# Merging the 32x32 blocks of four heads' triangular inverses at once

## The chip, the cores and the metric

The kernel runs on one core of one Trainium2 chip. The metric is device time in microseconds of one execution, the median of three runs: 887.85 us for the kernel before (886.28 to 888.44).

## The reference

One layer of a bidirectional encoder block, 512 tokens wide 1024, float32. An input projection gives pooling channels, q, k, v, gates and decays; branch A pools, branch B runs a chunked gated delta rule forward and backward for 8 heads of width 128; both are gated, summed, projected and added to x, and a channel mixer (up-projection, convolution, SiLU gate, down-projection) follows. What matters here is the triangular solve of the delta rule:

```python
L = jnp.where(strict, jnp.einsum('bhnid,bhnjd->bhnij', kb, k) * decay, 0.0)
eye = jnp.eye(CHUNK, dtype=L.dtype)
rhs = jnp.concatenate([kb * jnp.exp(G)[..., None], vb], axis=-1)
sol = lax.linalg.triangular_solve(L + eye, rhs, left_side=True, lower=True,
                                  unit_diagonal=True)
```

For each head, direction and chunk a unit triangular matrix is inverted and applied.

## The kernel before

**Chunks and heads.** The kernel uses chunks of 128 tokens (`NT` = 4 of them) instead of 64. The heads form two groups of `HG` = 4. For a group, one tile `nm` of shape (128, 4 heads, 2 directions, 4 chunks, 128) holds the triangular matrices; the solve multiplies by their inverses from there.

**The inverse in three levels.** `mats_unit` (L828) builds the matrices and writes their 32x32 diagonal blocks to DRAM; `inv_unit` (L864) inverts all of a group's blocks at once; `spread_unit` (L925) loads the inverted blocks back, into `nm` and, transposed, into a second tile `ext`. Then `merge_unit` (L949) merges 32x32 blocks to 64x64 (level 1) and 64x64 to 128x128 (level 2). An off-diagonal block of the inverse is a product of three blocks, so each level has two rounds of small float32 matmuls with a copy between:

- `m1` (PE, L960) writes bank `l1a`; `x1` (ACT, L964) copies it to SBUF.
- `m2` (PE, L971) writes bank `l1b`, copied back into `nm` by `k2a` (ACT, L982 and L983) and `k2b` (DVE, L987 and L988).
- `m2t` (PE, L978) makes the transposed product in bank `l1t`; `k2t` (ACT L992, DVE L994) puts it into `ext`.
- `m3` (PE, L1010 and L1011) writes `l2a`; `x2_` (ACT, L1015) copies it.
- `m4` (PE, L1021 and L1022) writes `l2b`; `k4` (ACT L1026, DVE L1028) copies it into `nm`.

The unit is called once for each head. Its small matmuls use 32x32 or 64x64 corners of the PE array, so those of different corners run side by side.

**What follows.** `delta_unit` (L1086) runs the recurrence for two heads at a time: `solve` (L1137) is its first PE step and needs both heads' finished `nm`; its scalings (L1141) write buffers of the ring `x4`, three of which the unit takes at its start. `fin_unit` finishes a head.

**Order.** The program is written as tasks with an engine, a cost, the names they read and write, and a key. `Planner.run` (L88) plays the tasks in time with these costs and gives the order of instructions. On each engine the ready task with the lowest key goes first. Dependences across engines add 0.5 us ahead of PE and 0.2 elsewhere. Large projections (three 128x512 matmuls for a step, L371 to L373, `mm3`) have late keys, so they fill PE wherever the chain of the delta rule (`CHAIN` keys) has nothing ready. Costs of ACT and DVE copies come from `ca` and `cd` (L188, L192). Each engine then runs its list in order and waits on semaphores. SP starts most transfers, ACT those of `ext`.

**Buffers.** `RINGS` (L243) gives the buffers of each kind: `ds` are 3 PSUM banks of 512 columns for the small steps, `x4` 3 SBUF tiles of 1024 columns (the blocks of `inv_unit`, the states of `delta_unit`), `x1` and `x2` one each for the copies in a merge. Rings in the strict list are taken in the order of declaration.

Of the kernel before, what the change touches and what calls it, by code (L numbers as in the profile page):

```python
# [209 lines left out]
def hybrid_block(  # L210
# [23 lines left out]
    pe, act, dve, pool, sp = nc.tensor, nc.scalar, nc.vector, nc.gpsimd, nc.sync  # L234
# [345 lines left out]
    def w_cols(c0, n=P):  # L580
        return w_in[0][:, c0 : c0 + n]
# [185 lines left out]
    nms, exts, vs = [None] * H, [None] * H, [None] * H  # L767
    nmg, extg = [None] * 2, [None] * 2
# [56 lines left out]
    def nmn(h):  # L825
        return [f"nm:{h // HG}#h{h}{d}" for d in range(2)]
# [119 lines left out]
            L(128, lambda b_=b_: load(b_, False), r=[f"uscr{g}", f"bscr{g}", f"nm:{g}"], w=[f"nml{g}#{b_}"], key=c, land=4.0, issue=1.1)  # L946


    def merge_unit(h):  # L949
        g, c = h // HG, CHAIN + 1000 * (h // HG) + 600 + 10 * h  # L950
        b = {}
        q = [slice(i * B32, (i + 1) * B32) for i in range(4)]
        lo_, hi_ = slice(0, 64), slice(64, 128)
        def m1():
            b["p1"] = bank("ds", f"l1a_{h}")[:, 0 : NT * B32].rearrange("p (t c) -> p t c", c=B32)
            nm, ext = nms[h], exts[h]
            a, z = slice(0, 32), slice(32, 64)
            for t in range(NT):
                for o, i, d, e in ((1, 0, 0, a), (3, 2, 0, a), (0, 1, 1, z), (2, 3, 1, z)):
                    pe.matmul(b["p1"][q[o], t, :], nm[q[i], d, t, q[o]], ext[q[i], d, t, e], start=True, stop=True)  # L960

        def x1():
            b["x1"] = ring("dp", "x1", (P, NT, B32), F32, f"x1_{h}")
            act.copy(b["x1"], b["p1"])  # L964

        def m2():
            p = b["p2"] = bank("ds", f"l1b_{h}")[:, 0 : NT * B32].rearrange("p (t c) -> p t c", c=B32)
            nm, x1_ = nms[h], b["x1"]
            for t in range(NT):
                for o, i, d in ((0, 1, 0), (2, 3, 0), (1, 0, 1), (3, 2, 1)):  # L970
                    pe.matmul(p[q[o], t, :], x1_[q[i], t, :], nm[q[i], d, t, q[i]], start=True, stop=True)  # L971

        def m2t():
            p = b["p2t"] = bank("ds", f"l1t_{h}")[:, 0 : NT * B32].rearrange("p (t c) -> p t c", c=B32)
            nm, x1_ = nms[h], b["x1"]
            for t in range(NT):
                for o, d in ((1, 0), (2, 1)):
                    pe.matmul(p[q[o], t, :], nm[q[o], d, t, q[o]], x1_[q[o], t, :], start=True, stop=True)  # L978

        def k2a():  # L980
            nm, p = nms[h], b["p2"]
            act.copy(nm[q[0], 0, :, q[1]], p[q[0]])  # L982
            act.copy(nm[q[2], 0, :, q[3]], p[q[2]])  # L983

        def k2b():
            nm, p = nms[h], b["p2"]
            dve.tensor_copy(nm[q[1], 1, :, q[0]], p[q[1]])  # L987
            dve.tensor_copy(nm[q[3], 1, :, q[2]], p[q[3]])  # L988

        def k2t(d):  # L990
            if d == 0:
                act.copy(exts[h][q[1], 0, :, 0:32], b["p2t"][q[1]])  # L992
            else:
                dve.tensor_copy(exts[h][q[2], 1, :, 32:64], b["p2t"][q[2]])  # L994

        nm_n, ext_n = nmn(h), [f"ext:{g}#{h}0", f"ext:{g}#{h}1"]
        M(0.75, m1, r=[*nm_n, *ext_n, f"exl{g}", f"nml{g}"], w=[f"ds:l1a{h}", f"x1:{h}"], key=c)
        A(ca(128), x1, r=[f"ds:l1a{h}"], w=[f"x1:{h}"], key=c)
        M(0.6, m2, r=[*nm_n, f"x1:{h}"], w=[f"ds:l1b{h}"], key=c)
        M(0.45, m2t, r=[*nm_n, f"x1:{h}"], w=[f"ds:l1t{h}"], key=c)  # L1000
        A(2 * ca(128), k2a, r=[f"ds:l1b{h}"], w=[nm_n[0]], key=c)
        V(2 * cd(128), k2b, r=[f"ds:l1b{h}"], w=[nm_n[1]], key=c)
        A(ca(128), lambda: k2t(0), r=[f"ds:l1t{h}"], w=[ext_n[0]], key=c)
        V(cd(128), lambda: k2t(1), r=[f"ds:l1t{h}"], w=[ext_n[1]], key=c)

        def m3():
            pv = b["p3"] = bank("ds", f"l2a_{h}")[:, 0:256].rearrange("p (t c) -> p t c", c=64)
            nm, ext = nms[h], exts[h]
            for t in range(NT):
                pe.matmul(pv[hi_, t, :], nm[lo_, 0, t, hi_], ext[lo_, 0, t, :], start=True, stop=True)  # L1010
                pe.matmul(pv[lo_, t, :], nm[hi_, 1, t, lo_], ext[hi_, 1, t, :], start=True, stop=True)  # L1011

        def x2_():
            b["x2"] = ring("dp", "x2", (P, NT, 64), F32, f"xl2_{h}")
            act.copy(b["x2"], b["p3"])  # L1015

        def m4():
            pv = b["p4"] = bank("ds", f"l2b_{h}")[:, 0:256].rearrange("p (t c) -> p t c", c=64)
            nm = nms[h]
            for t in range(NT):  # L1020
                pe.matmul(pv[lo_, t, :], b["x2"][hi_, t, :], nm[hi_, 0, t, hi_], start=True, stop=True)  # L1021
                pe.matmul(pv[hi_, t, :], b["x2"][lo_, t, :], nm[lo_, 1, t, lo_], start=True, stop=True)  # L1022

        def k4(d):
            if d == 0:
                act.copy(nms[h][lo_, 0, :, hi_], b["p4"][lo_])  # L1026
            else:
                dve.tensor_copy(nms[h][hi_, 1, :, lo_], b["p4"][hi_])  # L1028

        M(0.7, m3, r=[*nm_n, *ext_n], w=[f"ds:l2a{h}", f"x2:{h}"], key=c)  # L1030
        A(ca(256), x2_, r=[f"ds:l2a{h}"], w=[f"x2:{h}"], key=c)
        M(0.7, m4, r=[*nm_n, f"x2:{h}"], w=[f"ds:l2b{h}"], key=c)
        A(ca(256), lambda: k4(0), r=[f"ds:l2b{h}"], w=[nm_n[0]], key=c)
        V(cd(256), lambda: k4(1), r=[f"ds:l2b{h}"], w=[nm_n[1]], key=c)
# [388 lines left out]
    gbox, gpp, _ = job(w_cols(C_GATE, 32), KD, hx, hr, "gate", halves=True, pair=True)  # L1423
# [48 lines left out]
    x2 = [None] * NT  # L1472
# [214 lines left out]
    for c in range(NF):  # L1687
        b = {}
# [19 lines left out]
        else:  # L1708
            i = c - HK
# [255 lines left out]
```

## Time and profile before

| what | value |
|---|---|
| median of three runs | 887.85 us (886.28, 887.85, 888.44) |
| span of the profiled execution | 887.7 us (no other time of it is listed) |
| PE busy | 876.2 us, 99%, 5179 matmuls |
| DVE, ACT, POOL busy | 548.2, 462.1, 499.7 us |
| merges of group 0, first to last matmul and a little after | 163.7 to 188.1 us |
| merges of group 1 | 345.6 to 368.1 us |
| bytes read and written in HBM | 114.08 and 25.20 MB |

The profile is of one execution. Busy time counts instructions in flight; PE records matmuls, PEld weight loads, which overlap them. Matmuls are pipelined, so a large one shows 0.39 us while the next starts 0.23 us after it: durations on PE are read from start to start. A row of the timeline has start, duration, engine, line, operation, output and inputs, tile of the array, shape and count; brackets give the idle time before it and what ended that.

### The profile page before, as it was taken

What the parts mean: (1) busy time and instruction counts of PE and PEld (TensorE: products, weight loads), DVE (VectorE), ACT (ScalarE), POOL (GpSimd) and SP (SyncE); (2) the same over time, 40 slices, a digit from 0 to 9 for tenths busy, and PEclk for the clock granted to TensorE, in tenths of its full rate; (3) what the DMA queues carried; (4) which work ended last, traced back from release to release, by engine and by line L of the source; (5) the groups of instructions that cost most, each with busy time, mean ns of one, the idle gap of its engine ahead of it and who ended that gap; (6) DMA issues with size and microseconds to landing.
All of it is one profiled execution on the core that took longest, in us unless ns stands there. A gap on an engine that the chain in (4) does not pass through costs nothing. (4 is left out here: it accounts for less than half of the span.)

```text
span 887.7 us, 14092 instructions
## 1 busy us (share of the span) xinstructions
PE 876.2 (99%) x5179; PEld 737.7 (83%) x5179; DVE 548.2 (62%) x981; ACT 462.1 (52%) x791; POOL 499.7 (56%) x446
## 2 busy tenths in 40 slices
PE   8999999999999999999999999999999999999997
PEld 7988888788988887889878888888888888888886
DVE  5756687157777795555534244666655454569996
ACT  5688644435877444334854333444443333465664
POOL 3445555214556554243667905777788764567763
PEclk9999999999999999999999999999999999999999
DMA  7365545813344559112898606566766653366554
GB/s 207 87 204 141 131 120 163 148 25 112 91 134 117 143 148 150 43 49 81 254 291 265 191 21 210 194 215 218 241 214 202 236 168 100 115 194 197 167 172 159
DMA packets 176265, 140.20 MB, mean 158 GB/s; under 512 B 32110, under 2 KB 143547, under 8 KB 176196
## 3 DMA queue, kind: packets, MB, share of 16 engines
q1 hardware_dynamic: 167298, 137.20, 51.3%
q10 hardware_dynamic: 8898, 2.10, 1.6%
q8 instruction: 41, 0.67, 0.3%
q14 instruction: 28, 0.23, 0.1%
HBM read 114.08 MB, written 25.20 MB: 157 GB/s over the span
## 5 line engine op out<-in xcount | busy, mean ns | idle before, releaser
L396 POOL TENSOR_TENSOR wl_up<-wr_up,wh_up 128x512 fp32r<-128x512 f32 x88 | 115.0, 1328 | 49.3 <-ACT wh_up L392 49.2
L372 PE MATMUL ps_up<-h_lo,wh_up 128*128 128x512 f32 (+1 forms) x368 | 139.9, 380 | 0.3 <-DVE h_lo L541 0.3
L371 PE MATMUL ps_up<-h_hi,wh_up 128*128 128x512 f32 (+1 forms) x368 | 139.9, 380 | 0.0
L373 PE MATMUL ps_up<-h_hi,wl_up 128*128 128x512 f32 (+1 forms) x368 | 139.7, 380 | 0.0
L1678 DVE SCALAR_TENSOR_TENSOR c<-ps_up,fw,c 128x511 f32<-128x511 f32 x88 | 66.0, 750 | 100.0 <-ACT c L1672 94.1
L1663 POOL TENSOR_TENSOR tp<-tp 128x512 f32<-128x512 f32 x44 | 59.9, 1361 | 42.6 <-DMA tp<-in_ffn_down_dram 37.0
L1867 POOL TENSOR_TENSOR w_dn<-wr_dn,w_dn 128x512 fp32r<-128x512 f32 x44 | 66.1, 1515 | 28.5 <-ACT w_dn L1864 27.1
L372 PEld LDWEIGHTS ps_up<-h_lo,wh_up 128*128 128x128 f32 x368 | 69.2, 188 | 13.8 <-DVE h_lo L541 0.5
L373 PEld LDWEIGHTS ps_up<-h_hi,wl_up 128*128 128x128 f32 x368 | 69.2, 188 | 13.2
L371 PEld LDWEIGHTS ps_up<-h_hi,wh_up 128*128 128x128 f32 x368 | 69.2, 188 | 13.0
L392 ACT CAST wh_up<-wr_up 128x1024 fp32r<-128x1024 f32 x44 | 46.2, 1050 | 61.4 <-issue 29.3
L1864 ACT CAST w_dn<-wr_dn 128x512 fp32r<-128x512 f32 x69 | 42.4, 621 | 29.6 <-PE dn L373 21.1
L372 PE MATMUL dn<-w_dn,as 128*128 128x512 f32 x141 | 54.2, 385 | 0.0
L371 PE MATMUL dn<-w_dn,as 128*128 128x512 f32 x141 | 54.2, 384 | 0.0
L373 PE MATMUL dn<-w_dn,as 128*128 128x512 f32 x141 | 54.2, 384 | 0.0
L1632 DVE TENSOR_TENSOR as<-a,as 128x512 fp32r<-128x512 f32 (+1 forms) x41 | 41.8, 1044 | 0.1
L1628 ACT CAST as<-a 128x512 fp32r<-128x512 f32 (+1 forms) x41 | 21.5, 535 | 33.5 <-DVE a L1699 29.8
L396 POOL TENSOR_TENSOR wl_gp<-wr_gp,wh_gp 128x512 fp32r<-128x512 f32 x16 | 21.2, 1348 | 25.6 <-ACT wh_gp L392 25.6
L1672 ACT ACTIVATE c<-ps_up,fw 128x512 f32<-128x512 f32 x44 | 33.9, 770 | 0.0
L1701 ACT ACTIVATE c<-c 128x512 f32<-128x512 f32 x22 | 13.9, 633 | 35.0 <-DVE c L1678 35.0
L396 POOL TENSOR_TENSOR wl_do<-wr_do,wh_do 128x512 fp32r<-128x512 f32 x16 | 25.7, 1627 | 11.1 <-ACT wh_do L392 10.8
L396 POOL TENSOR_TENSOR wl_v<-wr_v,wh_v 128x512 fp32r<-128x512 f32 x16 | 20.5, 1304 | 19.8 <-ACT wh_v L392 19.8
(362 smaller groups left out, 2440.7 us busy)
## 6 DMA issues: line engine op xcount, KB each, us to landing
wr_up<-in_ffn_up_dram SPq DMA_DIRECT2D x44, 512.0 KB, 4.0
tp<-in_ffn_down_dram SPq DMA_DIRECT2D x22, 512.0 KB, 5.4
t_scr<-tp SPq DMA_DIRECT2D x44, 256.0 KB, 2.9
wr_dn<-t_scr SPq DMA_DIRECT2D x20, 512.0 KB, 3.9
wr_dn<-in_ffn_down_dram SPq DMA_DIRECT2D x15, 512.0 KB, 3.6
x<-in_x_dram SPq DMA_DIRECT2D x8, 512.0 KB, 5.4
wr_k<-in_w_in_dram SPq DMA_DIRECT2D x8, 512.0 KB, 6.5
wr_z<-in_w_in_dram SPq DMA_DIRECT2D x8, 512.0 KB, 3.9
```

Of the source, the lines that this page charges most:

```text
L371: pe.matmul(ps, ahi, bhi, start=first, stop=False)
L372: pe.matmul(ps, ahi, blo, start=False, stop=False)
L373: pe.matmul(ps, alo, bhi, start=False, stop=last)
L392: act.copy(b["hi"], b["raw"])
L396: pool.tensor_tensor(out=b["lo"][:, sl], in0=b["raw"][:, sl], in1=f32(b["hi"][:, sl]), op=ALU.subtract)
L1628: act.copy(sets[p][:, i : i + n, 0, :], src())
L1632: dve.tensor_tensor(out=w[:, :, 1, :], in0=src(), in1=f32(w[:, :, 0, :]), op=ALU.subtract)
L1663: G(cp(512), lambda o=o, x=x, y=y: pool.tensor_tensor(out=w(*o), in0=w(*x), in1=w(*y), op=ALU.subtract), r=[n(*x), n(*y)], w=[n(*o)], key=u)
L1672: act.activation(b[j], box["ps"], AF.Identity, scale=fw[:, 1, ci : ci + 1], bias=fw[:, 3, ci : ci + 1])
L1678: dve.scalar_tensor_tensor(out=y[:, lo:hi], in0=box["ps"][:, lo + sh : hi + sh], scalar=fw[:, k, ci : ci + 1], in1=y[:, lo:hi], op0=ALU.mu ...
L1864: act.copy(b["w"][:, 0, :], raw["t"][:, j, :])
L1867: eng.tensor_tensor(out=b["w"][:, 1, :], in0=raw["t"][:, j, :], in1=f32(b["w"][:, 0, :]), op=ALU.subtract)
```

## The change

`merge_unit` takes a group instead of a head. At level 1 the banks `l1a`, `l1t` and `l1b` hold all four heads (4 heads x 4 chunks x 32 columns = 512), and each of the steps is one PE task and one copy for each quadrant and direction. At level 2 a bank holds two heads (2 x 4 x 64 = 512), so `m3`, `x2_`, `m4` and `k4` run twice (`j` = 0, 1). `m2t` now stands ahead of `m2`. The copies `x1` and `x2_` write into one tile `mt` of the ring `x4` instead of tiles of their own; the ring `x1` goes, and `x2` serves `inv_unit` alone. Level 2's `m3` now names `ext` but not `nm` among what it reads. The matmuls are the same in number, shape and operands.

```diff
     RINGS = {
         "pp": 3, "ds": 3, "oo": 1, "raw": 3, "whi": 2, "wlo": 2, "y": 5, "f": 6, "z": 1, "q": 3, "v": 4,
-        "r4": 4, "nm": 1, "x4": 3, "qe": 4, "ext": 1, "x1": 1, "x2": 1, "xs": 2, "pw": 1, "pwr": 1, "cv3": 4, "sq2": 1, "as": 2, "tp": 1, "dhl": 3,
+        "r4": 4, "nm": 1, "x4": 3, "qe": 4, "ext": 1, "x2": 1, "xs": 2, "pw": 1, "pwr": 1, "cv3": 4, "sq2": 1, "as": 2, "tp": 1, "dhl": 3,
...
-    def merge_unit(h):
...
+        c = CHAIN + 1000 * g + 600
         b = {}
         q = [slice(i * B32, (i + 1) * B32) for i in range(4)]
         lo_, hi_ = slice(0, 64), slice(64, 128)
+        heads = range(HG)
+        nm_n = [[nmn(g * HG + j)[d] for j in heads] for d in range(2)]
+        ext_n = [[f"ext:{g}#{j // 2}{d}" for j in heads] for d in range(2)]
+        both = lambda n: n[0] + n[1]
+        def level1(name):
+            return bank("ds", f"{name}_{g}").rearrange("p (h t c) -> p h t c", h=HG, c=B32)
         def m1():
+            p = b["p1"] = level1("l1a")
+            nm, ext = nmg[g], extg[g]
             a, z = slice(0, 32), slice(32, 64)
+            for h in heads:
+                for t in range(NT):
+                    for o, i, d, e in ((1, 0, 0, a), (3, 2, 0, a), (0, 1, 1, z), (2, 3, 1, z)):
+                        pe.matmul(p[q[o], h, t, :], nm[q[i], h, d, t, q[o]], ext[q[i], h, d, t, e], start=True, stop=True)
         def x1():
+            b["mt"] = ring("dp", "x4", (P, 2, 512), F32, f"mt_{g}")
+            b["x1"] = b["mt"][:, 1].rearrange("p (h t c) -> p h t c", h=HG, c=B32)
             act.copy(b["x1"], b["p1"])
+        def m2t():
+            p = b["p2t"] = level1("l1t")
+            nm, x1_ = nmg[g], b["x1"]
+            for h in heads:
+                for t in range(NT):
+                    for o, d in ((1, 0), (2, 1)):
+                        pe.matmul(p[q[o], h, t, :], nm[q[o], h, d, t, q[o]], x1_[q[o], h, t, :], start=True, stop=True)
         def m2():
+            p = b["p2"] = level1("l1b")
+            nm, x1_ = nmg[g], b["x1"]
+            for h in heads:
+                for t in range(NT):
+                    for o, i, d in ((0, 1, 0), (2, 3, 0), (1, 0, 1), (3, 2, 1)):
+                        pe.matmul(p[q[o], h, t, :], x1_[q[i], h, t, :], nm[q[i], h, d, t, q[i]], start=True, stop=True)
         def k2t(d):
             if d == 0:
+                act.copy(extg[g][q[1], :, 0, :, 0:32], b["p2t"][q[1]])
             else:
+                dve.tensor_copy(extg[g][q[2], :, 1, :, 32:64], b["p2t"][q[2]])
+        def k2a(i):
+            act.copy(nmg[g][q[i], :, 0, :, q[i + 1]], b["p2"][q[i]])
+        def k2b(i):
+            dve.tensor_copy(nmg[g][q[i], :, 1, :, q[i - 1]], b["p2"][q[i]])
+        x1n = f"x4:mt{g}#1"
+        M(1.2, m1, r=[*both(nm_n), *both(ext_n), f"exl{g}", f"nml{g}"], w=[f"ds:l1a{g}"], key=c)
+        A(ca(512), x1, r=[f"ds:l1a{g}"], w=[x1n], key=c)
+        M(1.2, m2t, r=[*both(nm_n), x1n], w=[f"ds:l1t{g}"], key=c)
+        M(1.2, m2, r=[*both(nm_n), x1n], w=[f"ds:l1b{g}"], key=c)
+        A(ca(512), lambda: k2t(0), r=[f"ds:l1t{g}"], w=ext_n[0], key=c)
+        V(cd(512), lambda: k2t(1), r=[f"ds:l1t{g}"], w=ext_n[1], key=c)
+        for i in (0, 2):
+            A(ca(512), lambda i=i: k2a(i), r=[f"ds:l1b{g}"], w=nm_n[0], key=c + 5)
+            V(cd(512), lambda i=i: k2b(i + 1), r=[f"ds:l1b{g}"], w=nm_n[1], key=c + 5)
+        def level2(name, j):
+            return bank("ds", f"{name}_{g}{j}").rearrange("p (h t c) -> p h t c", h=2, c=64)
+        def m3(j):
+            p = b["p3", j] = level2("l2a", j)
+            nm, ext = nmg[g], extg[g]
+            for h in range(2):
+                for t in range(NT):
+                    pe.matmul(p[hi_, h, t, :], nm[lo_, 2 * j + h, 0, t, hi_], ext[lo_, 2 * j + h, 0, t, :], start=True, stop=True)
+                    pe.matmul(p[lo_, h, t, :], nm[hi_, 2 * j + h, 1, t, lo_], ext[hi_, 2 * j + h, 1, t, :], start=True, stop=True)
+        def x2_(j):
+            b["x2", j] = b["mt"][:, j].rearrange("p (h t c) -> p h t c", h=2, c=64)
+            act.copy(b["x2", j], b["p3", j])
+        def m4(j):
+            p = b["p4", j] = level2("l2b", j)
+            nm, x = nmg[g], b["x2", j]
+            for h in range(2):
+                for t in range(NT):
+                    pe.matmul(p[lo_, h, t, :], x[hi_, h, t, :], nm[hi_, 2 * j + h, 0, t, hi_], start=True, stop=True)
+                    pe.matmul(p[hi_, h, t, :], x[lo_, h, t, :], nm[lo_, 2 * j + h, 1, t, lo_], start=True, stop=True)
+        def k4(j, d):
+            hs = slice(2 * j, 2 * j + 2)
             if d == 0:
+                act.copy(nmg[g][lo_, hs, 0, :, hi_], b["p4", j][lo_])
             else:
+                dve.tensor_copy(nmg[g][hi_, hs, 1, :, lo_], b["p4", j][hi_])
+        for j in range(2):
+            hs = slice(2 * j, 2 * j + 2)
+            M(1.2, lambda j=j: m3(j), r=[*ext_n[0][hs], *ext_n[1][hs]], w=[f"ds:l2a{g}{j}", f"x4:mt{g}#{j}"], key=c + 10 + j)
+            A(ca(512), lambda j=j: x2_(j), r=[f"ds:l2a{g}{j}"], w=[f"x4:mt{g}#{j}"], key=c + 10 + j)
+        for j in range(2):
+            hs = slice(2 * j, 2 * j + 2)
+            M(1.2, lambda j=j: m4(j), r=[*nm_n[0][hs], *nm_n[1][hs], f"x4:mt{g}#{j}"], w=[f"ds:l2b{g}{j}"], key=c + 20 + j)
+            A(ca(512), lambda j=j: k4(j, 0), r=[f"ds:l2b{g}{j}"], w=nm_n[0][hs], key=c + 20 + j)
+            V(cd(512), lambda j=j: k4(j, 1), r=[f"ds:l2b{g}{j}"], w=nm_n[1][hs], key=c + 20 + j)
     def q_unit(h):
...
-    for h in range(HG):
-        merge_unit(h)
+    merge_unit(0)
...
-    for h in range(HG, H):
-        merge_unit(h)
+    merge_unit(1)
```

More of the change, by code (lines that the diff above doesn't have):

```diff
@@ L946, in spread_unit, with merge_unit @@
             L(128, lambda b_=b_: load(b_, False), r=[f"uscr{g}", f"bscr{g}", f"nm:{g}"], w=[f"nml{g}#{b_}"], key=c, land=4.0, issue=1.1)
-    def merge_unit(h):
-        g, c = h // HG, CHAIN + 1000 * (h // HG) + 600 + 10 * h
+    def merge_unit(g):
+        c = CHAIN + 1000 * g + 600
         b = {}
@@ L953, in merge_unit @@
         lo_, hi_ = slice(0, 64), slice(64, 128)
+        heads = range(HG)
[4 more added lines that the diff above has]
+            return bank("ds", f"{name}_{g}").rearrange("p (h t c) -> p h t c", h=HG, c=B32)
         def m1():
-            b["p1"] = bank("ds", f"l1a_{h}")[:, 0 : NT * B32].rearrange("p (t c) -> p t c", c=B32)
@@ L956, in m1 @@
-            nm, ext = nms[h], exts[h]
+            p = b["p1"] = level1("l1a")
+            nm, ext = nmg[g], extg[g]
             a, z = slice(0, 32), slice(32, 64)
-            for t in range(NT):
-                for o, i, d, e in ((1, 0, 0, a), (3, 2, 0, a), (0, 1, 1, z), (2, 3, 1, z)):
-                    pe.matmul(b["p1"][q[o], t, :], nm[q[i], d, t, q[o]], ext[q[i], d, t, e], start=True, stop=True)
+            for h in heads:
+                for t in range(NT):
+                    for o, i, d, e in ((1, 0, 0, a), (3, 2, 0, a), (0, 1, 1, z), (2, 3, 1, z)):
+                        pe.matmul(p[q[o], h, t, :], nm[q[i], h, d, t, q[o]], ext[q[i], h, d, t, e], start=True, stop=True)
@@ L962, in x1 @@
         def x1():
-            b["x1"] = ring("dp", "x1", (P, NT, B32), F32, f"x1_{h}")
+            b["mt"] = ring("dp", "x4", (P, 2, 512), F32, f"mt_{g}")
+            b["x1"] = b["mt"][:, 1].rearrange("p (h t c) -> p h t c", h=HG, c=B32)
             act.copy(b["x1"], b["p1"])
-        def m2():
[L967 to L988, printed above, removed]
+        def m2t():
[5 more added lines that the diff above has]
+                        pe.matmul(p[q[o], h, t, :], nm[q[o], h, d, t, q[o]], x1_[q[o], h, t, :], start=True, stop=True)
@@ L990, in k2t @@
+        def m2():
+            p = b["p2"] = level1("l1b")
[4 more added lines that the diff above has]
+                        pe.matmul(p[q[o], h, t, :], x1_[q[i], h, t, :], nm[q[i], h, d, t, q[i]], start=True, stop=True)
         def k2t(d):
             if d == 0:
-                act.copy(exts[h][q[1], 0, :, 0:32], b["p2t"][q[1]])
+                act.copy(extg[g][q[1], :, 0, :, 0:32], b["p2t"][q[1]])
@@ L993, in k2t @@
             else:
[L994 to L1022, printed above, removed]
@@ L1024, in k4 @@
-        def k4(d):
+                dve.tensor_copy(extg[g][q[2], :, 1, :, 32:64], b["p2t"][q[2]])
[7 more added lines that the diff above has]
+        M(1.2, m2t, r=[*both(nm_n), x1n], w=[f"ds:l1t{g}"], key=c)
@@ L1025, in k4 @@
+        def m4(j):
[7 more added lines that the diff above has]
+            hs = slice(2 * j, 2 * j + 2)
             if d == 0:
-                act.copy(nms[h][lo_, 0, :, hi_], b["p4"][lo_])
+                act.copy(nmg[g][lo_, hs, 0, :, hi_], b["p4", j][lo_])
@@ L1027, in k4 @@
             else:
[L1028 to L1034, printed above, removed]
+                dve.tensor_copy(nmg[g][hi_, hs, 1, :, lo_], b["p4", j][hi_])
@@ L1481, in merge_open @@
         pools["n2b"] = pools["xp"].tile([P, D], F32, tag="nb", name="n2b")
-    gone = [b for b in plan.owner if b.split(":")[0] in ("qe", "ext", "nm", "x1", "x2", "x4", "f", "z", "r4", "q", "v", "pw", "pwr")]
+    gone = [b for b in plan.owner if b.split(":")[0] in ("qe", "ext", "nm", "x2", "x4", "f", "z", "r4", "q", "v", "pw", "pwr")]
     Z(merge_open, w=["pool:xp"], after=gone)
```

## The prediction

> **What bounds the kernel now.** I read the page first: the busy times, then the DMA queues, which also carry the instructions.
>
> ```profile
> span 887.7 us, 14092 instructions
> PE 876.2 (99%) x5179; PEld 737.7 (83%) x5179; DVE 548.2 (62%) x981; ACT 462.1 (52%) x791; POOL 499.7 (56%) x446
> q8 instruction: 41, 0.67, 0.3%
> ```
>
> Then the busy time by stage:
>
> ```profile
> 163.69:188.07 24.38, 23.25 (x519) 18.39 (x519) 8.21 (x23) 10.52 (x29) 5.64 (x6) 1.00 0.29 85
> 345.60:368.10 22.50, 21.99 (x516) 17.29 (x515) 10.91 (x29) 10.19 (x30) 4.05 (x6) 1.00 0.28 72
> 182.00:440.00 258.00, 257.49 (x1871) 221.68 (x1871) 174.66 (x385) 143.47 (x260) 120.26 (x115) 1.00 0.42 111
> 440.00:500.00 60.00, 59.27 (x261) 48.62 (x260) 24.02 (x29) 31.06 (x45) 46.70 (x33) 1.00 0.80 259
> 600.00:700.00 100.00, 100.00 (x443) 82.81 (x442) 58.10 (x71) 41.81 (x59) 80.13 (x61) 1.00 0.66 218
> ```
>
> (Columns: length, then PE, PEld, DVE, ACT, POOL busy with counts, granted clock, DMA share, GB/s.) TensorE is never long without work, at full granted clock. So a microsecond of PE time saved or lost in a merge moves the end by about as much; time on ACT or DVE counts only where PE ends up waiting for it. The first two rows are the merges of the two groups (with some of the delta rule inside). A large 128x512 matmul takes 100/443 = 0.226 us there where nothing else runs.
>
> The merges themselves, in order of time on PE, group 1:
>
> ```profile
> 355.69 0.45 PE L971 MATMUL l1b<-nm,x 32*32 32x32 f32 x32
> 356.07 0.27 PE L1021 MATMUL l2b<-nm,xl 64*64 64x64 f32 x1
> ...
> 356.18 0.22 PE L1021 MATMUL l2b<-nm,xl 64*64 64x64 f32 x1
> 356.24 0.22 PE L1021 MATMUL l2b<-nm,xl 64*64 64x64 f32 x1
> ...
> 356.53 0.22 PE L1022 MATMUL l2b<-nm,xl 64*64 64x64 f32 x1
> 356.68 0.44 PE L978 MATMUL l1t<-x,nm 32*32 32x32 f32 x16
> 357.05 0.50 PE L371 MATMUL ps_gp<-h_hi,wh_gp 128*128 128x512 f32 x1
> ...
> 357.94 0.45 PE L960 MATMUL l1a<-ext,nm 32*32 32x32 f32 x32
> ```
>
> From start to start: l1b 0.38, l2b 0.61, l1t 0.37 us, and three large matmuls 0.89 us where three cost 0.68 elsewhere: each return from small matmuls to large ones costs 0.21 us. (l1a is like l1b, l2a like l2b. Each float32 matmul appears as two records, each with a weight load.)
>
> **The change, part by part.** It removes no matmul. It removes bursts: 40 PE steps become 14, 48 ACT copies 16, 32 DVE copies 10.
>
> *Fixed cost of a burst.* Where l1b and l1t of one head follow each other they take 0.64 us together, against 0.38 + 0.37 apart:
>
> ```profile
> 166.13 0.42 PE L971 MATMUL l1b<-nm,x 32*32 32x32 f32 x28
> ...
> 166.40 0.44 PE L978 MATMUL l1t<-x,nm 32*32 32x32 f32 x15
> 166.77 0.50 PE L371 MATMUL ps_k<-h_hi,wh_k 128*128 128x512 f32 x1
> ```
>
> So a 32x32 burst has a fixed part of 0.11 us and 0.27 us per head. A 64x64 burst is 8 pairs 0.058 us apart (356.18 to 356.24), plus 0.15. Before, four heads: 4 x (0.38 + about 0.70 + 0.61 + 0.61) = 9.2 us. After: l1a 0.11 + 4 x 0.27 = 1.19; l1t and l1b together 0.11 + 4 x 0.53 = 2.23; l2a and l2b twice each, 16 x 0.058 + 0.15 = 1.08, so 4.32; sum 7.74. Gain 1.5 us a group, 2.9 in both.
>
> *Returns to large matmuls.* In group 1 seven groups of three stand between the bursts, each opened by one of these:
>
> ```profile
> L371 PE MATMUL ps_gp<-h_hi,wh_gp 128*128 128x512 f32 x7 | 3.4, 481 | 0.0
> ```
>
> I take seven for both groups. After the change there are about four places where the chain must wait for copies and the planner fills in large ones (after l1a, l1b, l2a, l2b). Three fewer by 0.21 is 0.6 a group, 1.3 in both.
>
> *Stalls that go.* Two lie in the merges:
>
> ```profile
> 173.61 0.38 PE L971 MATMUL l1b<-nm,x 32*32 32x32 f32 x21
> 174.89 0.31 PE L971 MATMUL l1b<-nm,x 32*32 32x32 f32 x11 [0.91 <-issue]
> 353.80 0.45 PE L960 MATMUL l1a<-ext,nm 32*32 32x32 f32 x32 [0.45 <-DVE nm L988]
> 163.69 0.26 PE L960 MATMUL l1a<-ext,nm 32*32 32x32 f32 x6
> 164.16 0.43 PE L960 MATMUL l1a<-ext,nm 32*32 32x32 f32 x26 [0.22 <-DMA ext<-e_scr]
> ```
>
> I count 0.91 + 0.45 = 1.4 us as gone; the wait at 164.16 for the loads stays. Gains so far: 2.9 + 1.3 + 1.4 = 5.6 us.
>
> *What takes the place of the 0.91.* That stall is the odd row: a half-done loop of one step, no engine named, PE simply had no instruction. Queue q8 brings instructions: 41 packets of 16 KB for 2 x 5179 = 10358 PE records, one for each 253 or so, thus 256 instructions of 64 bytes. Counting back and forth from the stall in steps of 256 records gives block boundaries:
>
> ```profile
> 164.31:169.66 5.35, 5.35 (x144) 3.79 (x139) 0.87 (x3) 2.72 (x7) 2.52 (x2) 1.00 0.76 248
> 169.66:174.89 5.23, 4.32 (x139) 3.15 (x136) 1.30 (x4) 2.14 (x7) 0.00 (x0) 1.00 0.40 103
> 174.89:347.61 172.72, 172.72 (x1139) 148.26 (x1141) 126.58 (x285) 99.17 (x181) 83.56 (x75) 1.00 0.46 114
> 347.61:351.23 3.62, 3.62 (x131) 2.66 (x135) 2.45 (x5) 1.30 (x5) 2.52 (x2) 1.00 0.24 56
> ```
>
> (The third is nine blocks; instructions that straddle an edge are counted on both sides.) One q8 packet starts in 172.2 to 172.5 and one in 348.2 to 348.5, the first and second row here:
>
> ```profile
> q8 instruction: 1, 0.02, 22.2%
> q8 instruction: 1, 0.02, 24.2%
> ```
>
> As shares of 16 engines for 0.3 us they took 1.07 and 1.16 us. My reading: on entering a block PE fetches the next one, and it waits if 256 instructions are done before that has come. In the stalled case a block took 5.2 us, with DMA busy (share 0.76 in the block before); the packet landed near 173.4 and PE went on 1.5 us later. Where the queues were calm, the packet came 0.7 us after the boundary at 347.61; 0.7 + 1.2 + 1.5 = 3.4 us a block, and the block of 3.62 us shows no stall, which is consistent. Bounds: nothing (if the reading is wrong) and 5.2 us. I take 3.4, near the unstalled 3.62, and 5.2 only for the first block of group 0, which has the traffic of 164 to 169 as now.
>
> A merged l1a is 4 x 32 records with their loads, 256 instructions in 1.19 us; l1t and l1b are 384 in 2.23. Between them the planner, which charges 1.2 us for the step, 0.64 for the copy and 0.7 of slack, has room for two groups of three large matmuls, 1.57 us with the return, 12 instructions.
> Group 0: boundary at 164.3, some 50 records into l1a; l1a ends 165.3, l1t starts 166.9, the next boundary is due at 167.1, its block is there at 164.3 + 5.2 = 169.5: stall 2.4. The 256 instructions then take 1.5 us, the next block 3.4: stall 1.9. After that come three large matmuls, l2a and three more, over 4 us for a block: none.
> Group 1: boundary 87 records after its start at 345.60, at 346.0; l1t starts 348.4, the next boundary is due 348.8, the block there at 349.4: 0.6. Then again 3.4 - 1.5 = 1.9.
> Sum 6.8 us. In terms of the time L per block: 2.4 + (L - 1.5) + (L - 2.8) + (L - 1.5).
>
> *Copies.* They lie off PE's path, and DVE follows ACT on one bank:
>
> ```profile
> L983 ACT COPY nm<-l1b 32x128 f32<-32x128 f32 x4 | 1.0, 257 | 0.0
> L1202 ACT COPY sgd<-ps_gd 128x512 f32<-128x512 f32 x1 | 0.6, 578 | 0.0
> L1141 DVE TENSOR_TENSOR rw<-pw,bkd 128x512 f32<-128x512 f32 x1 | 0.7, 692 | 1.1 <-PE pw L1137 1.1
> DVE nm L987 <- ACT nm L983: 21.7, 5, 15.1
> DVE nm L1028 <- ACT nm L1026: 10.5, 5, 3.6
> ```
>
> The merged ones have 512 columns: 0.58 on ACT; on DVE 0.69 at most. If they alternate on the l1b bank, 2 x 0.58 + 2 x 0.69 = 2.5 us pass instead of the planned 1.5. Behind that waits only l2b, and l2a (2.16 us) and the large matmuls lie between, so I cost it at nothing. If that cover is gone it is 1.0 us a group. [...]
>
> *Other queues and the chain.* SP and POOL get nothing new. The tile `mt` holds an x4 buffer that the first delta unit opens; it is free after the second l2b, 1.1 us after the first, before the delta rule's first scaling. The delta rule starts later than now by no more than the stalls' sum; the large matmuls from 182 to 440 (257.49 of 258 us busy) cover it. At 440 to 500 the idle 0.73 us could grow by about 1 us; kept for the range.
>
> **Sum.** 5.6 gained, 6.8 lost: 1.2 us slower. The profiled span is 887.7, 0.15 below the median of 887.85 (no other time of that execution is listed), so 889.0.
>
> **The rivals.**
> Faster: instructions are never late, and the 0.91 was something else. For it: it is the only such stall in 888 us. Against it: it stands inside one step, after the densest stretch, on no wait. Then all 5.6 stays: 882.2. [...]
> Slower: a block takes 5.2 us throughout, as when DMA is busy. Then the loss is 2.4 + 3.7 + 2.4 + 3.7 = 12.2, net 6.6: 894.5. Against it stands the block of 3.62 us without a stall. It decides from L = 3.9 us, where 3L - 3.4 = 8.3 is 2.7 above the gain.
> Alternating copies uncovered, instructions on time: 5.6 - 2.0, 884.3. For it: the waits of L987 and L1028 on ACT. Against it: PE has other work there. [...]
>
> **How the numbers follow.** 0.3% is 2.7 us, about what a measurement of this kernel can tell from no change. Forecast (L from about 2.5 to 3.9; 886 to 890.4) 0.45; instructions on time 0.30; copies uncovered 0.05; slower with L above 3.9 0.20. So faster 0.35, same 0.45, slower 0.20. The range 881.5 to 892.0 leaves out under 0.1 on each side (L above 4.3, and a gain over 6.3); the forecast's own is 886 to 891.
>
> **What would show it.** Right: PE rows inside l1t and l1b split by stalls of 0.5 to 2.5 us with "issue" as releaser and no engine named, two a group; q8 packets a few us apart there; returns of 0.21 fewer; the span of burst records near 1.2 and 2.2 us without the stalls; ACT and DVE counts lower by 32 and 22. Wrong: bursts of 384 records without a gap, both merges together some 5 us shorter. Also wrong if PE waits there name ACT or DVE copies, or if the planner's new order opens gaps after 440 us, which I can't see from here.

## The result and the profile after

The changed kernel takes 895.0 us, the median of four runs (893.35 to 896.24), against 888.14 (886.28 to 888.93) for the kernel before on the same chip: a ratio of 1.0081, 95% interval 1.0064 to 1.0098. It is 0.8% slower, clear of the spread of the runs; 889.0 was forecast, and 895.0 lies 3.0 us above the range. The profiled execution has a span of 894.4 us against 887.7, so 6.7 us are to be found.

The page of after, its head:

```profile
span 894.4 us, 14017 instructions
PE 875.3 (98%) x5179; PEld 739.8 (83%) x5179; DVE 551.0 (62%) x959; ACT 454.8 (51%) x757; POOL 499.5 (56%) x446
PEclk9999999899999999899999999999999999999999
```

PE's busy time fell by 0.9 us (876.2 before), its idle time rose from 11.5 to 19.1 us. The counts of ACT and DVE are 34 and 22 lower (32 and 22 were forecast). New are the two slices where the granted clock is 8 instead of 9. The waits of PE after (us in total, times, longest), the largest of them and two smaller ones:

```profile
PE l1b L990 <- issue: 4.1, 2, 2.5
PE l1t L982 <- issue: 3.5, 2, 2.2
PE pt_v L776 <- ACT cv_v L761: 1.4, 1, 1.4
PE pms L1269 <- DVE osl L1264: 0.7, 1, 0.7
PE pms L1268 <- DVE nm L845: 0.5, 1, 0.5
```

And before, those that went:

```profile
PE l1b L971 <- issue: 0.9, 1, 0.9
PE ps_do L372 <- POOL o_lo L1270: 0.7, 1, 0.7
PE l1a L960 <- DVE nm L988: 0.5, 1, 0.5
```

The "issue" waits, in which no engine and no transfer is named, grew from 0.9 to 7.6 us, all inside `l1t` and `l1b`. Three waits outside the merges are new, on steps that the change does not touch: `pt_v` (at 272 us) and `pms` (at 277 and 444 us), 2.6 us together. The timeline of PE in group 0 and then in group 1 shows the stalls in place:

```profile
166.53 0.50 PE L982 MATMUL l1t<-mt,nm 32*32 32x32 f32 x18
169.25 1.02 PE L982 MATMUL l1t<-mt,nm 32*32 32x32 f32 x41 [2.22 <-issue]
...
172.98 0.86 PE L990 MATMUL l1b<-nm,mt 32*32 32x32 f32 x46 [1.54 <-issue]
173.76 0.80 PE L371 MATMUL ps_k<-h_hi,wh_k 128*128 128x512 f32 x1
...
354.32 0.47 PE L982 MATMUL l1t<-mt,nm 32*32 32x32 f32 x17 [1.23 <-issue]
...
358.33 0.53 PE L990 MATMUL l1b<-nm,mt 32*32 32x32 f32 x22 [2.54 <-issue]
```

Two stalls a group, as forecast. An instruction packet of 16 KB belongs to each: one of queue q8 starts in 166.6 to 166.9, in 170.6 to 170.9, in 351.7 to 352.0 and in 355.4 to 355.7 us, in this order:

```profile
q8 instruction: 1, 0.02, 24.0%
q8 instruction: 1, 0.02, 19.1%
q8 instruction: 1, 0.02, 24.6%
q8 instruction: 1, 0.02, 29.2%
```

As shares of 16 engines for 0.3 us they took 1.15, 0.92, 1.18 and 1.40 us, and PE went on 1.3 to 1.4 us after each had landed (at 167.84, 171.64, 353.03 and 356.90 us). (In before, the packet of the one stall landed at 173.35 us and PE went on at 174.89, 1.5 us later.) But look at the first large matmul behind the pair of group 0: 0.80 us, where it took 0.50 at such a place before. The windows view says why (length, then PE, PEld, DVE, ACT, POOL busy with counts, granted clock, DMA share, GB/s):

```profile
166.30:169.73 3.43, 1.21 (x50) 0.87 (x50) 0.00 (x0) 1.02 (x2) 2.48 (x2) 1.00 0.28 96
169.73:176.55 6.82, 5.28 (x181) 4.34 (x176) 2.07 (x3) 1.73 (x3) 0.00 (x0) 0.50 0.30 82
354.04:357.46 3.42, 1.46 (x128) 1.35 (x128) 0.69 (x1) 1.19 (x2) 2.25 (x2) 1.00 0.38 92
357.46:364.29 6.83, 5.96 (x78) 4.87 (x80) 1.38 (x2) 2.32 (x4) 0.23 (x3) 0.50 0.23 74
```

Behind a stretch of 3.4 us in which PE was busy for only 1.2 to 1.5 us, the granted clock is 0.50 for 6.83 us, and PE is slower in it: the three to six large matmuls there start 0.43 us apart (0.23 at full clock), the pairs of `l2a` 0.11 us (0.06). The kernel before has no such window between 12.7 and 886.5 us. The price stood in no term of the forecast.

### The profile page after: what moved, and what is told of

Same layout as the page of the kernel before. It is cut to its first block, busy times and chain, and to the rows that moved or that the text cites. A ratio compares the mean times of both kernels' runs of the same rounds, so it can differ in the third digit from the quotient of the medians.

```text
span 894.4 us, 14017 instructions
## 1 busy us (share of the span) xinstructions
PE 875.3 (98%) x5179; PEld 739.8 (83%) x5179; DVE 551.0 (62%) x959; ACT 454.8 (51%) x757; POOL 499.5 (56%) x446
## 4 chain that ended last, share of the span: by engine, by line
PE 94%; DVE 3%; issue 1%; ACT 1%; DVEq 0%; ACTq 0%
PE ps_up L373 9%; PE ps_up L372 9%; PE ps_up L371 9%; PE dn L372 4%; PE dn L373 4%; PE dn L371 4%; PE ps_k L371 2%; PE ps_gp L371 2%; PE ps_gp L373 2%; PE ps_gp L372 2%; PE ps_k L373 2%; PE ps_k L372 2%; PE ps_wo L371 2%; PE ps_wo L372 2%; PE ps_wo L373 2%; PE ps_z L372 2%
## 5 line engine op out<-in xcount | busy, mean ns | idle before, releaser
L396 POOL TENSOR_TENSOR wl_k<-wr_k,wh_k 128x512 fp32r<-128x512 f32 x16 | 20.2, 1283 | 28.7 <-ACT wh_k L392 16.8
L751 DVE SCALAR_TENSOR_TENSOR cv_q<-ps_q,cw,cv_q 128x510 f32<-128x510 f32 (+1 forms) x32 | 23.9, 748 | 13.4 <-ACT cv_q L745 12.6
```

The lines of the kernel that those rows point to most:

```text
L396: pool.tensor_tensor(out=b["lo"][:, sl], in0=b["raw"][:, sl], in1=f32(b["hi"][:, sl]), op=ALU.subtract)
L751: dve.scalar_tensor_tensor(out=y[:, lo:hi], in0=box["ps"][:, lo + sh : hi + sh], scalar=cw[:, k, ci : ci + 1], in1=y[:, lo:hi], op0=ALU.mu ...
```

## The experiments

Three theories went into the first four runs: the stalls are the loss; the clock behind them is a second loss; the planner's new order is a third, independent of both.

**Moving the block boundaries, first way.** After, with 24 dummy matmuls among the warm-up matmuls at the start, 96 PE instructions with unused results, so that each block of 256 ends 96 instructions earlier in the work:

```diff
+        for i in range(24):
+            pe.matmul(pt[0:32, 0:32], ones[0:32, 0:32], ones[0:32, 0:32], start=True, stop=True)
```

> The changed kernel with 24 tiny 32x32 matmuls (96 recorded PE instructions) added to the warm-up at the start, so that every later block boundary falls 96 instructions earlier in the work. Theory (instructions arrive in blocks of 256): the stalls move with the boundary. Group 0: no longer after 18 matmul records of l1t and 82 of l1b, but after about 104 records of l1a (0 to 0.6 us) and about 34 of l1b (1 to 2.5 us). Group 1: just ahead of l1t, among the large matmuls (1 to 2 us), and after about 58 records of l1b (2 to 3 us). Rival (a run of small matmuls may only be so long, or copies are late): the stalls stay after the same numbers of records as in the changed kernel. Time within 2 us of the changed kernel either way.

Measured: span 888.6, the one time 890.6 (before: 888.34 in this set). The waits of this kernel on "issue":

```profile
PE l1b L992 <- issue: 1.1, 2, 0.9
PE l2a L1026 <- issue: 0.5, 1, 0.5
```

Of the stalls that the theory listed, the two in `l1b` came after 34 of its matmul records in group 0 and after 58 in group 1, exactly as expected; the rival had them stay at their old places. They were smaller than expected (0.2 and 0.9 us), the other two did not show, 0.5 us came at `l2a`, and the time, expected within 2 us of after's, is 4.4 us below it. The same matmuls in the same order have 6.0 us of stalls less (1.6 instead of 7.6, and some gaps too short for the list) only because the boundaries lie elsewhere. The clock stayed full in both merges. The waits of `pt_v` and `pms` stayed. The shift had a price of its own, though: the dummies ran from 5.88 to 7.51 us, the clock was at half for 10.24 us behind them (8.99 to 19.23) instead of 3.41, and equal instructions came 3.3 us later than in before. How much of the half clock is owed to the dummies stays open: two later profiles with nothing added there have 6.83 us of it at the start. The shift had to be made elsewhere (below).

**One level alone.** Only level 1 merged for four heads, level 2 for each head as before:

```diff
-            M(1.2, lambda j=j: m3(j), r=[*ext_n[0][hs], *ext_n[1][hs]], w=[f"ds:l2a{g}{j}", f"x4:mt{g}#{j}"], key=c + 10 + j)
...
+            M(0.7, m3, r=[*nm_h, *ext_h], w=[f"ds:l2a{h}", f"x2:{h}"], key=c + 10 + 10 * (h % HG))
...
+        for h in range(g * HG, (g + 1) * HG):
+            level2(h)
```

> Level 1 for four heads at once as in the changed kernel, level 2 head by head as before. Theory: the dense stretch is l1a, l1t, l1b (640 instructions), and it is all there, so PE idle with no engine named stays at 6 to 8 us, the clock is halved twice for about 7 us, and the time is 892 to 897 us. Rival (level 2 with two heads in a bank, or its copies, costs the time): the stalls mostly go, 884 to 888 us.

Measured 902.38 us, ratio 1.0162 (1.0143 to 1.0181). `l1t` and `l1b` wait 3.5 us each on "issue". Two stretches of it:

```profile
170.12:176.95 6.83, 5.33 (x129) 4.42 (x114) 2.07 (x3) 1.73 (x3) 0.00 (x0) 0.50 0.29 82
364.68:371.51 6.83, 5.07 (x56) 4.14 (x56) 1.78 (x3) 1.74 (x3) 0.00 (x0) 0.50 0.14 41
```

Stalls of 7.0 us and two half-clock windows, as in after: both belong to level 1. It is even slower than after, and than the 892 to 897 us expected: PE's busy time is 880.4 us. The bursts of level 2 are many again, and nine or ten large matmuls stand in each slow window, where after has three and six. The order again brings waits that before has not: `pt_v` on DVE and `ps_gp` on ACT 1.1 us each, `ps_do` on POOL 1.0.

**The other level alone.** Level 1 for each head, level 2 for two heads at once (the mirror image of that diff).

> Level 2 for two heads at once as in the changed kernel, level 1 head by head as before. Theory: no burst is dense enough, stalls with no engine named stay below 1.5 us in all, the clock stays full, and the time is 885 to 888.5 us, a little below the kernel before. Rival (level 2 is at fault): stalls and halved clock as in the changed kernel, 890 us or more.

Measured 892.11 us, ratio 1.0041 (1.0024 to 1.0057). No "issue" wait above 0.3 us, no slow clock, and still 3.8 us slower than before in this set. The theory's 885 to 888.5 us is missed, and what its rival gave as the reason is not there. PE has waits that neither before nor after has: `ps_p` on ACT 1.1 us, `ks` on ACT 1.0, `ps_do` on POOL 1.0, `o` on DVE 0.8. These steps are not in the merge either. So a new order of the merges' tasks, by itself, costs a few us elsewhere. And PE's busy time is 876.2 us, as in before: level 2 alone saved none, though the forecast's sum has 1.1 us of bursts for it.

**Cutting the bursts.** After, with `l1a` and `l1b` cut into two heads each, and planner tasks without instructions between them that keep 1.9 us free for large matmuls, so that 256 instructions take longer than a block:

```diff
-        M(1.2, m2, r=[*both(nm_n), x1n], w=[f"ds:l1b{g}"], key=c)
+        gap(1.9, f"ds:l1t{g}", f"gapb{g}")
+        M(0.65, lambda: m2(range(2)), r=[..., f"gapb{g}"], w=[f"ds:l1b{g}#0"], key=c)
+        gap(1.9, f"ds:l1b{g}#0", f"gapc{g}")
+        M(0.65, lambda: m2(range(2, 4)), r=[..., f"gapc{g}"], w=[f"ds:l1b{g}#1"], key=c)
```

> The changed kernel with the same banks and copies, but l1a and l1b each cut in two steps of two heads, and a planned pause of 1.9 us between the steps, which the planner fills with large matmuls; the same small matmuls at under 256 instructions per 5 us. Theory: stalls below 1 us in all, full clock, and what the change saves is left: 882.5 to 886 us. Rival (the merged copies or waits cost the time, not instruction supply): 890 to 896 us, PE waiting for ACT or DVE copies.

Measured 891.21 us, ratio 1.0033 (1.0018 to 1.0048). That is not the 882.5 to 886 us of the theory but inside the rival's range, and PE does wait for ACT and DVE, though not for the merged copies. No stall in either merge, full clock there. Ahead of group 1's merges it runs 3.3 us earlier than before at the same instruction; at the end it is 2.0 us later. Of the 5.3 us lost between, 3.4 are waits at 398 to 407 us: `o` for ACT and DVE (0.9 and 0.8), `ks` and `ps_pw` for 0.5 to 0.7 each. There the clock falls too, with no "issue" wait near:

```profile
402.57:405.98 3.41, 1.66 (x9) 1.15 (x9) 1.64 (x3) 3.40 (x7) 1.84 (x2) 1.00 0.62 201
405.98:409.40 3.42, 3.06 (x14) 3.06 (x15) 1.13 (x5) 2.39 (x5) 0.08 (x1) 0.50 0.14 55
```

So a half clock can follow idleness of PE that no instruction block made.

**The block by itself.** The kernel before, with bursts of 16 to 256 dummy matmuls (64 to 1024 PE instructions) in the channel mixer, where only large matmuls stand around:

```diff
+            n = {2: 16, 4: 32, 6: 64, 8: 96, 10: 128, 13: 192, 16: 256}.get(c, 0)
+            if j == 1 and n:
+                M(0.11 + 0.017 * n, lambda c=c, n=n: burst(c, n), r=[pp], w=[f"ds:bu{c}"], key=u + 8)
```

> The kernel before, with seven bursts of dummy 32x32 float32 matmuls added between up-projections of the channel mixer (about 550 to 740 us, only large matmuls around, DMA share about 0.66): 16, 32, 64, 96, 128, 192 and 256 matmuls, four PE instructions each, so 64 to 1024 instructions. Their results are not used; the output is the same as before. By the block theory (a block of 256 instructions takes 3.7 to 5 us to come, measured from the boundary before): no stall in the bursts of 64 to 256 instructions, one stall of 2 to 3 us at most in that of 384, and in those of 512, 768 and 1024 a stall at each boundary at PE record indexes a multiple of 256 apart, in phase with all earlier stalls (index 193 modulo 256), so that the longest burst takes about 15 to 19 us instead of its own 4.4; and, if a stall of this kind halves the granted clock, windows of 0.50 of 3.4 to 6.8 us behind the long bursts. [...] Rival B, a limit on the length of a run of small matmuls: stalls at a fixed count from the start of each burst, whatever the index.

Measured 928.42 us (one time), span 926.7. The bursts of 512, 768 and 1024 instructions on PE's timeline (a matmul of the list stands for two instructions):

```profile
659.01 1.99 PE L1693 MATMUL bu<-ones 32*32 32x32 f32 x213
664.33 0.85 PE L1693 MATMUL bu<-ones 32*32 32x32 f32 x43 [3.33 <-issue]
700.26 1.84 PE L1693 MATMUL bu<-ones 32*32 32x32 f32 x194
705.75 1.93 PE L1693 MATMUL bu<-ones 32*32 32x32 f32 x128 [3.65 <-issue]
709.75 1.07 PE L1693 MATMUL bu<-ones 32*32 32x32 f32 x62 [2.08 <-issue]
745.30 1.67 PE L1693 MATMUL bu<-ones 32*32 32x32 f32 x175
749.55 1.27 PE L1693 MATMUL bu<-ones 32*32 32x32 f32 x128 [2.59 <-issue]
754.65 1.93 PE L1693 MATMUL bu<-ones 32*32 32x32 f32 x128 [3.83 <-issue]
758.38 1.29 PE L1693 MATMUL bu<-ones 32*32 32x32 f32 x81 [1.80 <-issue]
```

The window behind the first stops of the longest:

```profile
751.87:762.11 10.24, 5.66 (x215) 4.98 (x215) 0.00 (x0) 0.00 (x0) 0.00 (x0) 0.50 0.03 8
```

Bursts up to 384 run through without a stop. From 512 on they stop, and between two stops stand 128 matmuls each time, which is 256 instructions. The first stop comes after 426, 388 and 350 instructions of its burst: not at a fixed length, which rules out a limit on the burst. From resume to resume a block takes 4.00, 5.10 and 3.73 us here, 3.73 and 4.01 us in after (169.25 to 172.98, 354.32 to 358.33) and 3.45 us in group 1 of the version with the planner's true costs (357.31 to 360.76). Counted over all instructions of PE from the start of the program (those that only wait on a semaphore too), the first one after every stop here has an index of 193 modulo 256, and so do the stall of the kernel before and all four of after (1985 and 2241 in group 0, 4801 and 5057 in group 1). The three long bursts are followed by half clock of 6.83, 10.24 and 10.24 us (the last row). This fits two blocks at hand at most, since each of the three long bursts stopped after 426 instructions or fewer, and one more every 3.45 to 5.1 us. The longest burst took 14.3 us (745.30 to the next large matmul at 759.60) instead of its own 4.4, a little less than the 15 us expected at least.

**Moving the boundaries, second way.** After, with the 96 dummy instructions in a step that runs at 39.9 us, at full clock, in four corners of the array:

```diff
+            for i in range(24):
+                o, k = ((0, 1), (2, 3), (1, 0), (3, 2))[i % 4]
+                ...
+                pe.matmul(pg[o, 192 + i // 4 * 32 : 224 + i // 4 * 32], ones[k, 0:B32], ones[k, 0:B32], start=True, stop=True)
```

> The kernel after, with 24 dummy 32x32 matmuls (96 PE instructions, results unused) added near 25 us, at full clock: every later block boundary lies 96 instructions earlier in the work, and the planner's order stays that of after. By the theory that after lost 6.7 us to block stalls and 4.8 to the halved clock behind them: the stalls fall to about 1.6 us, the clock stays full in the merges, and the time is 885 to 888; the waits of pt_v and pms (1.4 and 1.2 us) stay, since they belong to the order. Rival, the loss of after is in the planner's order: the time stays at 893 to 896.

Measured 887.6 us median, ratio to before 0.9991 (0.9980 to 1.0003), where after has 1.0081. Its waits on "issue", and the stretch between the same two instructions around each group's merges, first in after (group 0, group 1), then here:

```profile
PE l1b L994 <- issue: 1.2, 2, 0.6
PE l2a L1028 <- issue: 1.0, 1, 1.0
```

```profile
163.73:182.50 18.77, 15.01 (x473) 12.69 (x473) 3.46 (x5) 6.17 (x10) 3.52 (x4) 0.82 0.31 96
348.74:372.86 24.12, 20.35 (x499) 17.27 (x499) 10.29 (x19) 8.14 (x14) 4.34 (x6) 0.86 0.28 75
164.59:180.01 15.42, 13.21 (x473) 11.14 (x472) 3.46 (x5) 6.19 (x10) 3.53 (x4) 1.00 0.42 126
346.24:364.58 18.34, 17.70 (x499) 15.16 (x499) 10.27 (x19) 8.16 (x14) 4.34 (x6) 1.00 0.37 97
```

This is after with 2.2 us of stalls instead of 7.6 and full clock, and it gives the two prices that after mixes. The same matmuls keep PE busy for 15.01 - 13.21 = 1.80 and 20.35 - 17.70 = 2.65 us longer in after: the half clock cost 4.5 us. Without it after's PE busy time would be 875.3 - 4.5 = 870.8 us, so the merging saved 876.2 - 870.8 = 5.4 us of busy time. (The busy times of the two pages differ by only 3.5 us, because the dummies take 0.7 us here, and the first 39 us keep PE busy 0.3 us longer.) `pt_v` and `pms` wait as in after.

**Cut in group 0, merged in group 1.** Group 0 as in the cut version, group 1 as in after, with the 96 dummy instructions at 39.9 us (no new lines beyond the last two diffs):

> Group 0's level-1 merges cut into steps of two heads, with gaps for large matmuls between them, group 1 as in after, and the 96 dummy PE instructions near 25 us. Theory (block stalls, then the halved clock): no stall in either group, full clock, the gain of about 5 us of the merging kept: 882 to 885, if the planner's order opens no new waits of more than 1 us; 885 to 888 with waits as in the version where both groups were cut. Rival (the merging is worth nothing by itself): 888 to 890.

Measured 886.93 us, ratio 0.9986 (0.9975 to 0.9997). Stalls 0.9 us, no slow window after the start; `pt_v` waits 0.2, and `pms` no longer, but `ps_do` waits 1.0 for POOL, as in the cut version, and `l1a` 0.9 for its loads.

It is the best of all versions, 0.7 us ahead of the shifted kernel and 1.2 of before, under the 0.3% that count. The expected 882 to 885 was missed; 885 to 888, expected with waits as in the cut version, holds. With group 0 cut, part of the bursts' saving is gone again (busy 874.1 us, with 6.83 us of half clock at the start instead of 3.41 in that profile).

**The same without the dummies.**

> As the version in which group 0 is cut and group 1 merged as in after, but without the 96 dummy PE instructions: the same steps in the same order, only the block boundaries lie 96 instructions later in the work. Theory (stalls where 256 instructions run in less than a block takes to come, and a halved clock when PE idles 1.5 us or more of a 3.41 us window): nothing changes in group 0; in group 1 the stalls come back as in after (1.2 and 2.5 us instead of 0.3 and 0.6), and with them one window of half clock of 6.83 us, about 2 us more: 4 to 5 us longer than the version with the dummies, so 890.5 to 892. Rival (the dummies or their place near 25 us matter in another way, the phase does not): within 1 us of 886.9.

Measured 888.65 us, ratio 1.0006 (0.9995 to 1.0017), 1.7 us more than with them; against before, which took 888.52 us in this set and 888.08 in that one, 1.3 us more. That lies between the two ranges on record: the theory's is missed, and so is the rival's. Group 1 on PE's timeline, and two windows of 3.41 us there:

```profile
353.06 0.91 PE L987 MATMUL l1t<-mt,nm 32*32 32x32 f32 x45 [0.95 <-issue]
...
356.95 0.64 PE L997 MATMUL l1b<-nm,mt 32*32 32x32 f32 x51 [2.24 <-issue]
```

```profile
354.46:357.87 3.41, 1.17 (x84) 0.98 (x71) 0.92 (x2) 0.80 (x2) 0.00 (x0) 1.00 0.00 0
357.87:361.28 3.41, 3.41 (x49) 2.76 (x49) 1.15 (x2) 1.58 (x3) 0.00 (x0) 0.50 0.02 5
```

The stalls and the half clock are back in group 1 and only there, so the phase decides where they fall. The size was expected at 4 to 5 us: of that the stalls are 2.3 (3.2 against 0.9), the clock fell for one window of 3.41 us instead of 6.83, the dummies' own 0.7 us are saved, and `l1a` waits 0.2 instead of 0.9 us for its loads.

**The planner told the truth.** After, with the costs of the merge steps set to their measured length:

```diff
-        M(1.2, m2t, r=[*both(nm_n), x1n], w=[f"ds:l1t{g}"], key=c)
-        M(1.2, m2, r=[*both(nm_n), x1n], w=[f"ds:l1b{g}"], key=c)
+        M(3.4, m2t, r=[*both(nm_n), x1n], w=[f"ds:l1t{g}"], key=c)
+        M(3.9, m2, r=[*both(nm_n), x1n], w=[f"ds:l1b{g}"], key=c)
...
```

> The kernel after, with the planner's costs of the merge steps set to their measured length (l1a 1.25, l1t 3.4, l1b 3.9 with their stalls, l2a 1.3, l2b 1.05). If the waits of pt_v and pms (2.6 us together) come from a plan that has the merges end 4 us too early, they go and the time falls to 891 to 893, with the stalls and the halved clock as in after. If they come from the order in which the merging lets the delta rule's steps follow, whatever the costs, they stay, or others of 1 us take their place: 894 to 896.

Measured 895.53 us, ratio 1.0079 (1.0060 to 1.0097): no gain.

Of the three waits outside the merges only that on `osl` (0.7) went; `pt_v` waits 1.4 and `pms` 0.5 as in after, and the stalls are 7.6 again. A plan that has the merges end too early is not what makes the other two.

## Why the prediction was wrong

Its sum was 5.6 us gained and 6.8 lost. By the runs, against the 6.7 us between the spans:

| term | forecast | measured | from |
|---|---|---|---|
| fewer bursts, fewer returns | -2.9 - 1.3 = -4.2 | -5.4 | PE busy of before, and of after at full clock |
| stalls that go | -1.4 | -1.4 | `l1b` 0.9 and `l1a` 0.5 of before |
| waits for blocks | +6.8 | +7.6 | `l1t` 3.5, `l1b` 4.1 |
| half clock behind them | none | +4.5 | the same stretches, after against shifted |
| waits by the new order | none in the sum | +1.9 | `pt_v` 1.4, `pms` 1.2, less `ps_do` 0.7 |
| sum | +1.2 | +7.2 | 6.7 between the spans; rest 0.5 |

**The savings** were sized a little low. Of the parts that can be read at full clock in the shifted kernel, group 1's `l1a` took 1.21 us (346.24 to the next large matmul at 347.45), forecast 1.19, and its `l2a` 2.16, as forecast; how the 5.4 us divide between bursts and returns was not measured.

**The blocks** were read right from one row of 0.91 us and a queue of 41 packets. The three parts of a block's time, 0.7 us to the packet, 1.2 for it and 1.5 behind it, came as 1.5, 0.9 and 1.3 us in group 0 and as 1.2, 1.4 and 1.4 in group 1 (from one resume to the next). The four stalls were put at 2.4, 1.9, 0.6 and 1.9 and came as 2.22, 1.54, 1.23 and 2.54. The formula 3L - 3.4 with 7.6 gives L = 3.7 us instead of 3.4, inside the forecast's own band (2.5 to 3.9); in group 0's second stall the half clock also slowed the 256 instructions (2.19 us busy instead of the 1.5 forecast), which left less to wait. A sum with 7.6 would still have come to 2.0 us slower, 889.8: the mis-sized L is not what failed.

**The copies** cost nothing, as the sum had it: no wait of PE inside the merges names ACT or DVE, so that rival is out. The rival with instructions on time is out by the dummy bursts, of which the three longest stopped after 426, 388 and 350 instructions. The rival that was nearest in time (894.5, L = 5.2 throughout) gave the right time for the wrong reason: the blocks of after that can be read from resume to resume took 3.73 and 4.01 us (169.25 to 172.98 and 354.32 to 358.33 above), and the stalls came to 7.6 us, not 12.2.

**The step that failed** is the treatment of a stall as time lost once. The forecast laid two stalls a group, 4.3 and 2.5 us, into some 5 us, and never asked what PE's idleness does to the clock; it had read only that the clock was 1.00 in every row of before. Behind the stalls the clock was 0.50 for 6.83 us, twice. The profile of before shows it at its ends alone: the clock is at half for 3.41 us at the start, and again from 886.5 us, behind 3.41 us in which PE does nothing. In after the slow windows begin at 9.30, 169.73 and 357.46 us, 47 and 55 times 3.413 us apart, and the first lasts 3.413 us, the others twice that. PE need not be idle throughout ahead of the fall: it was busy for 1.21 and 1.46 us of the 3.4 us ahead of the second and the third. That the stalls cause it is shown by the shifted kernel: with the same matmuls and 2.2 us of stalls the clock stays full.

**The second miss** is smaller: the sum has nothing for waits that a new order opens between 182 and 440 us, where it trusted the large matmuls to cover all. `pt_v` waits 1.4 us at 272 us, in the middle of that stretch, and does so in every version with after's order, with stalls or without. The forecast had kept about 1 us for later gaps, at 440 to 500 us, where one of the two waits of `pms` came (0.7). What in the order makes these waits stays open: the versions with other orders have others in other places (1 to 5 us in all), and true costs for the merge steps remove one of three.

Where the gain went, then: 5.4 + 1.4 us were gained, 1.2 more than forecast. The same stretch lost 7.6 to blocks and 4.5 to the clock, and the order 1.9. With most of the block stalls and the slow clock gone (the shifted kernel) the merging comes out about even with before (0.9991), not 5.6 us ahead: 2.2 us of stalls were still there, the order took 1.9, the dummies 0.7, and `l1a` waited 0.4 us longer for its loads.

## What to carry to other kernels

Small matmuls put side by side use up instructions faster than they come (`l1a` 256 in 1.2 us, where a block came every 3.45 to 5.1 us): count PE instructions, and where a second boundary of 256 would be reached less than some 4 us after the first (my estimate from those times), a stop there is likely. When a forecast puts a stall into PE's time, look at the 3.41 us around it: windows in which PE was busy for 1.17 to 1.90 us were followed by half clock in the merges and bursts here, and it cost 4.5 us on top of 7.6. To see what a merged step is worth by itself, shift the block boundaries with a few unused instructions, away from the start of the kernel, and compare PE's busy time between the same instructions.

## What the runs showed of the hardware

- The half clock follows a window of 3.41 us in which PE is busy in part: 1.21 and 1.46 us of it in after's merges, 1.90 and 1.61 with level 1 alone (166.71 to 170.12, 361.27 to 364.68), 1.17 in the version without the dummies, 1.28 and 1.27 in the dummy bursts (659.72 to 663.13, 748.46 to 751.87), 1.66 in the cut version. No sharp threshold can be read. A window with 1.93 us (the start of the longest dummy burst) was not followed by half clock; one with 2.33 us, nearly all of it small matmuls, was (in the version with the planner's true costs). At the end of the kernel, where only large matmuls stand, one with 1.52 us was followed by it (level 2 alone) and one with 1.56 us was not (the bursts). In this order:

```profile
745.04:748.46 3.42, 1.93 (x177) 1.57 (x176) 1.44 (x2) 1.73 (x2) 2.12 (x2) 1.00 0.50 144
355.03:358.44 3.41, 2.33 (x156) 1.90 (x158) 0.11 (x1) 1.69 (x3) 2.70 (x3) 1.00 0.03 8
883.11:886.52 3.41, 1.52 (x13) 1.32 (x11) 2.13 (x9) 1.03 (x4) 0.00 (x0) 1.00 0.44 165
919.13:922.54 3.41, 1.56 (x13) 1.34 (x12) 2.12 (x9) 1.02 (x5) 0.00 (x0) 1.00 0.45 166
```

- A PE that looks busy is not always enough. With the dummies at the start, this window shows PE busy throughout, nearly all of it with the 32x32 matmuls in one corner of the array and with matmuls of one row (`n1b`), and the clock was at half (0.50 from 8.99 to 19.23 us) behind it:

```profile
5.57:8.98 3.41, 3.41 (x55) 2.44 (x54) 0.16 (x1) 2.02 (x6) 0.97 (x2) 1.00 1.15 318
```

- A block of 256 PE instructions takes 3.45 to 5.1 us from stop to stop. The share of busy DMA engines does not order these times: 3.73 us at a share of 0.02, 5.10 at 0.36, 4.00 at 0.98:

```profile
754.65:758.38 3.73, 1.93 (x128) 1.80 (x128) 0.00 (x0) 0.00 (x0) 0.00 (x0) 0.50 0.02 4
749.55:754.65 5.10, 1.27 (x128) 1.17 (x128) 0.72 (x2) 0.00 (x0) 0.00 (x0) 0.73 0.36 106
705.75:709.75 4.00, 1.93 (x129) 1.79 (x128) 0.00 (x0) 0.00 (x0) 0.00 (x0) 0.50 0.98 292
```

The forecast had put the difference between 3.4 and 5.2 us down to DMA traffic; these rows do not bear that out.
